# PEER on one Trainium2 core: one instruction for both one-hot matrices, one for both weighted parts, and u summed in PSUM

## The chip, the cores and the metric

The kernel runs on one core of a Trainium2 chip. The metric is the device time of one execution in microseconds (us). Before the change the median of three runs is 2842.26 us (2841.84 to 2842.48).

## The reference, cut to what matters

Two transformer blocks follow each other; the second one ends each of its two layers with PEER, a mixture of 16384 one-row experts. The change lies there.

```python
def peer(h, w_q, sub_keys, u_tab, v_tab):
    xt = h.reshape(-1, PEER_TOKENS, D)
    def chunk_fn(xc):
        T = xc.shape[0]
        q = (xc @ w_q).reshape(T, PEER_HEADS, 2, PEER_QDIM // 2)
        s = jnp.einsum('thcd,hcnd->thcn', q, sub_keys, preferred_element_type=f32)
        sv, si = lax.top_k(s, PEER_TOPK)
        comb = (sv[:, :, 0, :, None] + sv[:, :, 1, None, :]).reshape(T, PEER_HEADS, PEER_TOPK * PEER_TOPK)
        cv, ci = lax.top_k(comb, PEER_TOPK)
        i1 = jnp.take_along_axis(si[:, :, 0], ci // PEER_TOPK, axis=-1)
        i2 = jnp.take_along_axis(si[:, :, 1], ci % PEER_TOPK, axis=-1)
        eidx = i1 * PEER_NKEYS + i2
        w = jax.nn.softmax(cv, axis=-1)
        u = u_tab[eidx]
        a = jax.nn.gelu(jnp.einsum('td,thkd->thk', xc, u, preferred_element_type=f32)) * w
        return jnp.einsum('thk,thkd->td', a.astype(v_tab.dtype), v_tab[eidx])
    return lax.map(chunk_fn, xt).reshape(B, S, D)
```

There are 256 tokens, a model width of 1024, 8 heads, 128 keys for each half and 16 picks a head.

## The kernel before, in words

Weights are streamed. `Stream` loads granules of 128 x 1024 fp32 numbers (512 KB, four raw buffers) over SP's queue. For each granule ACT rounds to fp32r (`wh`, L279), and DVE subtracts to get the rest (`wl`, L284); four such pairs are held, so both run up to three granules ahead of PE. Every product is made of three: wh with the high part of x, wh with the low part, wl with the high part. `Stream.block` hands PE a block and, at the first block of a granule, calls `tick` (one step of each background generator in `bg`), then `ahead` (conversions that are due), then `run_posts` (what was put off to the next granule). That order is the order in DVE's, ACT's and PE's queues; nothing else schedules.

PEER gathers no expert. It computes gelu(u x) for all 16384 experts, in 128 chunks of 128 experts, multiplies by a dense weight W that is zero where an expert was not picked, and multiplies by v, in 128 chunks. Each chunk of u or v is one granule. One layer runs in these stretches (in brackets their begin in layer 0, in us):

- queries and scores, and then `route` as a background generator: top 16 of 128, top 16 of the sums, indices, softmax. Its end writes the tables `i1T`, `i2T`, `wT`, each number twice side by side, tokens along the free axis.
- u chunks 0 to 63 into `G0` (991.6), with `route` still in the background.
- u chunks 64 to 97 into `G1` (1185.2), with `w_gen(0)` in the background.
- v group "a", 30 chunks of `G0` (1308.0).
- u chunks 98 to 127 into `G0` (1391.7), no generator beside them.
- v group "b", 34 chunks (1474.9), with `w_gen(1)` in the background.
- v groups "c" and "d", 64 chunks (1598.0).

`u_chunks` multiplies a chunk by all 256 tokens: for each of 8 blocks a matmul of wh with the high and low parts side by side (512 columns, L1670) and one of wl with the high part (256 columns, L1671). The low sums stand in the other half of the PSUM bank. ACT copies them to `G` (L1675), DVE adds the high half (L1678), and after every second chunk ACT makes the gelu in place (L1681). The two PSUM banks of `pu` (and two of `px` in the first stretch) hold one chunk each and come free with the add.

`w_gen(part, ...)` makes W for 64 of the 128 values of the second key, eight tokens to a tick, 32 ticks and one to end. A tick's `product` (16 small matmuls, L1709) multiplies the one-hot matrix `A` of the first key by the weighted one-hot matrix `B` of the second, in two fp16 parts; `scale` (L1716) multiplies the result of the tick before into `G`; `build` makes E and A by comparing a row of numbers with the tables (L1697, L1698), then the two parts of B (L1701).

`v_chunks` splits two columns of G into a high and a low part (L552 on ACT, L553 `gl` on DVE) and runs 12 matmuls of 512 columns a chunk (L1765). The constant EARLY (34) says how many u chunks run before group "a" and how many v chunks group "b" has.

`lin_t` (L433 to L435) multiplies other layers' weights in three matmuls of 256 columns, wh and wl each under a load of its own; its moving operand in the first MLP is the same tile `x` that u uses.

Of the kernel before, what the change touches and what calls it, by code (L numbers as in the profile page):

```python
# [34 lines left out]
EARLY = 34  # L35
# [293 lines left out]
class TileSum:  # L329
# [35 lines left out]
class Kern:  # L365
# [867 lines left out]
    def ret(self):  # L1233
# [3 lines left out]
        with tc.tile_pool(name="ret", bufs=1, reuse_waits="tile") as mp:  # L1237
            tab = mp.tile([P, 2048], F32, name="tab")
# [221 lines left out]
    def peer(self, layer):  # L1460
# [26 lines left out]
        sv, si = [], []
        for b in range(2):
            t = tp.tile([P, 16, TOPK], F32, name=f"sv{b}")
            sv.append(t)  # L1490
            t = tp.tile([P, 16, TOPK], U32, name=f"si{b}")
            si.append(t)
# [40 lines left out]
        def tile2(shape, dt, name):  # L1533
            r = []
            for b in range(2):
                t = tp.tile(shape, dt, name=f"{name}{b}", bufs=1)
                r.append(t)
            return r

        def route():  # L1540
# [15 lines left out]
            comb = tile2([P, 8, 112], F32, "comb")  # L1556
            sif = tile2([P, 16, TOPK], F16, "sif")
            cv = tile2([P, 8, TOPK], F32, "cv")
            ci = tile2([P, 8, TOPK], U32, "ci")
# [650 lines left out]
```

## Time and profile before

| | before |
|---|---|
| median of 3 runs | 2842.26 us |
| the profiled execution | 2838.77 us |
| its span, first to last instruction | 2837.1 us |
| PE busy | 2729.0 us, 96% |
| PE weight loads busy | 2369.2 us, 84% |
| DVE busy | 2236.7 us, 79% |
| ACT busy | 1485.1 us, 52% |
| POOL busy | 271.4 us, 10% |
| chain that ended last | PE 59%, DVE 33%, issue 5%, ACT 2% |

The profile is one execution. A matmul's duration in it reaches from its start to its modelled end; matmuls overlap, so what one costs is the distance from its start to the next start. On DVE too the next instruction can start a little before the end shown for the one before it. PE's busy share says little for the same reason; the granted clock is at its full level, 2.4 GHz, in all the stretches named above.

### The profile page before, as it was taken

The page shows a single profiled execution, that of the slowest core. Times are in us where ns is not written, and L with a number is a line of the kernel's source. Part 1 is how long each engine was busy: PE and PEld are TensorE (multiplying, and loading weights), DVE is VectorE, ACT ScalarE, POOL GpSimd, SP SyncE. Part 2 cuts the span into 40 slices and gives each one's busy share as a digit, 9 for nine tenths or more (in the row PEclk, how much of TensorE's full clock was granted, in tenths as well). Part 3 has the DMA queues.
Part 4 walks back from the last instruction along what each step waited for, and adds up shares of the span by engine and source line. Part 5 has one row for each costly group of instructions (what it writes and reads, how often), then busy time and mean ns, then how long its engine had stood idle before and what let it go on. Part 6 is the DMA issues. An engine that isn't in the chain of part 4 may idle for free.

```text
span 2837.1 us, 46836 instructions
## 1 busy us (share of the span) xinstructions
PE 2729.0 (96%) x17758; PEld 2369.2 (84%) x17758; DVE 2236.7 (79%) x4398; ACT 1485.1 (52%) x2411; POOL 271.4 (10%) x262
## 2 busy tenths in 40 slices
PE   8999999999999999999999999899999999999998
PEld 7889899898999878888887788778878888877786
DVE  7868977788768899797569755887999895579655
ACT  6557545674545554644553444665546544543444
POOL 2010013000202303000000000212203000000001
PEclk9999999999999999999999999999999999999999
DMA  5648976588554455545554555423455546544663
GB/s 197 223 151 301 320 275 233 183 311 303 188 164 155 138 168 172 185 142 179 188 176 142 178 187 191 131 91 110 132 169 183 168 147 193 186 157 142 192 187 110
DMA packets 143406, 521.04 MB, mean 184 GB/s; under 512 B 15919, under 2 KB 17229, under 8 KB 142669
## 3 DMA queue, kind: packets, MB, share of 16 engines
q1 hardware_dynamic: 142893, 515.96, 55.0%
q8 instruction: 139, 2.28, 0.3%
q10 hardware_dynamic: 288, 2.10, 0.2%
q14 instruction: 86, 0.70, 0.1%
HBM read 516.95 MB, written 1.05 MB: 183 GB/s over the span
## 4 chain that ended last, share of the span: by engine, by line
PE 59%; DVE 33%; issue 5%; ACT 2%; POOL 0%; DMA 0%; SPq 0%; DVEq 0%; ACTq 0%; POOLq 0%
PE vo L1765 18%; DVE wl L284 12%; PE u L1670 6%; PE lin L434 5%; PE lin L433 5%; PE lin L435 5%; PE lin L497 4%; DVE B L1701 3%; PE u L1671 3%; DVE G L1716 3%; PE lin L498 2%; DVE G L1678 2%; DVE E L1697 1%; PE lin L537 1%; PE lin L536 1%
## 5 line engine op out<-in xcount | busy, mean ns | idle before, releaser
L284 DVE TENSOR_TENSOR wl<-raw,wh 128x1024 fp32r<-128x1024 f32 x861 | 1083.8, 1262 | 312.4 <-ACT wh L279 311.8
L279 ACT ACTIVATE wh<-raw 128x1024 fp32r<-128x1024 f32 x861 | 909.9, 1058 | 567.6 <-PE vo L1765 403.4
L1670 PE MATMUL u<-x,wh 128*128 128x512 f32 x2048 | 729.6, 399 | 7.4 <-DVE rawb L1406 0.2
L1671 PE MATMUL u<-x,wl 128*128 128x256 f32 x2048 | 577.0, 282 | 15.0 <-DVE wl L284 13.4
L1670 PEld LDWEIGHTS u<-x,wh 128*128 128x128 f32 x2048 | 384.2, 188 | 101.3 <-DVE G L1678 14.7
L1671 PEld LDWEIGHTS u<-x,wl 128*128 128x128 f32 x2048 | 386.2, 189 | 27.4 <-DVE wl L284 27.2
L1765 PE MATMUL vo<-wh,gl 128*128 128x512 f32 x1008 | 319.3, 398 | 3.8
L1765 PE MATMUL vo<-wh,gh 128*128 128x512 f32 x1008 | 321.2, 400 | 0.0
L1765 PE MATMUL vo<-wl,gh 128*128 128x512 f32 x1008 | 316.0, 394 | 0.0
L433 PE MATMUL lin<-x,wh 128*128 128x256 f32 x920 | 271.0, 295 | 1.9 <-ACT x L555 1.5
L434 PE MATMUL lin<-x,wh 128*128 128x256 f32 x920 | 261.7, 284 | 1.0 <-DVE x L556 0.9
L435 PE MATMUL lin<-x,wl 128*128 128x256 f32 x920 | 260.9, 284 | 0.0
L1765 PEld LDWEIGHTS vo<-wh,gl 128*128 128x128 f32 x1008 | 187.5, 188 | 58.6 <-DVE gl L553 16.9
L1765 PEld LDWEIGHTS vo<-wl,gh 128*128 128x128 f32 x1008 | 189.8, 188 | 44.2
L1765 PEld LDWEIGHTS vo<-wh,gh 128*128 128x128 f32 x1008 | 184.9, 189 | 38.7
L1681 ACT ACTIVATE G<-G 128x512 f32<-128x512 f32 x128 | 80.6, 630 | 229.9 <-DVE G L1678 229.9
L433 PEld LDWEIGHTS lin<-x,wh 128*128 128x128 f32 x920 | 177.4, 193 | 4.0 <-ACT x L555 1.9
L434 PEld LDWEIGHTS lin<-x,wh 128*128 128x128 f32 x920 | 177.4, 193 | 3.1 <-DVE x L556 1.8
L348 POOL TENSOR_TENSOR acc<-sq 128x256 f32<-128x256 f32 x17 | 15.4, 907 | 1690.4 <-ACT sq L337 1690.4
L435 PEld LDWEIGHTS lin<-x,wl 128*128 128x128 f32 x920 | 177.1, 193 | 0.0
L497 PE MATMUL lin<-y,wh 128*128 128x512 f32 x496 | 174.2, 393 | 0.0
L1675 ACT COPY G<-u 128x256 f32<-128x256 f32 x256 | 93.5, 365 | 147.8 <-PE u L1671 147.8
(550 smaller groups left out, 4823.0 us busy)
## 6 DMA issues: line engine op xcount, KB each, us to landing
raw<-in_peer_u SPq DMA_DIRECT2D x256, 512.0 KB, 3.5
raw<-in_peer_v SPq DMA_DIRECT2D x256, 512.0 KB, 3.6
adaw<-in_ada SPq DMA_DIRECT2D x112, 512.0 KB, 6.1
raw<-in_mlp_in SPq DMA_DIRECT2D x64, 512.0 KB, 4.6
raw<-in_mlp_out SPq DMA_DIRECT2D x64, 512.0 KB, 5.4
raw<-in_peer_q SPq DMA_DIRECT2D x32, 512.0 KB, 3.5
raw<-in_sb_qk SPq DMA_DIRECT2D x16, 512.0 KB, 3.7
raw<-in_ret_g SPq DMA_DIRECT2D x16, 512.0 KB, 3.5
```

The costliest lines, as they stand in the source:

```text
L279: k.nc.scalar.activation(h, raw, AF.Copy)
L284: k.nc.vector.tensor_tensor(l, raw, h.bitcast(F32), op=ALU.subtract)
L433: mm(ps, wh, xh, start=start, stop=False)
L434: mm(ps, wh, xl, start=False, stop=False)
L435: mm(ps, wl, xh, start=False, stop=stop)
L497: mm(ps, wh, hl[:, i], start=i == 0, stop=False, **kw)
L1670: mm(p, wh, hx[:, i], start=i == 0, stop=False, skip_group_check=True)
L1671: mm(p[:, 0, :], wl, hh[:, i, :], start=False, stop=i == KT - 1, skip_group_check=True)
L1675: nc.scalar.copy(g, p[:, 1, :])
L1701: nc.vector.tensor_tensor(B[:, j], E, row(wT[:, j, ts, :], PART), op=ALU.mult)
L1716: nc.vector.scalar_tensor_tensor(g, pc[:, c0:c0 + m, :], 1.0 / W_SCALE, g, op0=ALU.mult, op1=ALU.mult)
L1765: mm(vo[2 * b + e], x[:, j, t], w[:, e * 512:(e + 1) * 512], start=fst and m == 0, stop=bool(lst) and m == 2)
```

## The change

- In `u_chunks` the matmul of 512 columns becomes two of 256 with the same weights, and all three add up in the same 256 columns. A PSUM bank now holds two chunks. The copy and the add are gone; the gelu reads PSUM and writes `G`.
- In `w_gen` one comparison makes A and E, as 192 columns for each token: the numbers 0 to 127 and the 64 of the part, against a table `iT` with the first index twice and the second once. One product makes both parts of B, and one `scale` covers all 64 rows also for part 1.
- `G` is one tile of 100 rows; G1 is its first 36, G0 the other 64. EARLY is 36. The routing's tables lie in G1's rows until u is written there.
- The buffers of the running sums (`sq`, `acc`) move to a pool `sums`, which each stage sets.

```diff
-EARLY = 34
+EARLY = 36
...
-        self.iota2 = cp.tile([P, P // 2, 2], F16, name="iota2")
-        nc.vector.tensor_copy(self.iota2.rearrange("p a b -> p (a b)"), self.c("iota"))
+        self.iota3 = cp.tile([P, 2, 3 * PART], F16, name="iota3")
+        for part in range(2):
+            nc.vector.tensor_copy(self.iota3[:, part, :P], self.c("iota"))
+            nc.vector.tensor_copy(self.iota3[:, part, P:], self.c("iota")[:, part * PART:(part + 1) * PART])
...
-        G0 = gp.tile([P, PART, S], F32, name="G0")
+        G = gp.tile([P, EARLY + PART, S], F32, name="G")
+        G0, G1 = G[:, EARLY:, :], G[:, :EARLY, :]
         rt = es.enter_context(tc.tile_pool(name="route", bufs=1, reuse_waits="tile"))
 
-        i1T = rt.tile([P, S, 2], F16, name="i1T")
-        i2T = rt.tile([P, S, 2], F16, name="i2T")
-        wT = rt.tile([P, 2, S, 2], F16, name="wT")
+        iT = rt.tile([P, S, 3, 2], F16, name="iT")
+        wT = rt.tile([P, S, 2, 2], F16, name="wT")
...
+        flat, room = G1.rearrange("p c s -> p (c s)"), [0]
+
+        def table(shape, dt):
+
+            n = math.prod(shape[1:])
+            words = n // 2 if dt == F16 else n
+            t = flat[:, room[0]:room[0] + words]
+            room[0] += words
+            if dt != F32:
+                t = t.bitcast(dt)
+            if len(shape) == 2:
+                return t
+            d = " ".join("abc"[:len(shape) - 1])
+            return t.rearrange(f"p ({d}) -> p {d}", **dict(zip("abc", shape[1:])))
+
+        sv = [table([P, 16, TOPK], F32) for b in range(2)]
...
-                nc.scalar.copy(i1T[:, cols, :], twice(t[:, 0:P]))
-                nc.scalar.copy(i2T[:, cols, :], twice(t[:, P:2 * P]))
-                ws = tp.tile([P, P], F32, name="af0", bufs=1)
+                for i, x in enumerate((t[:, 0:P], t[:, 0:P], t[:, P:2 * P])):
+                    nc.scalar.copy(iT[:, cols, i, :], twice(x))
+                ws = f[b]
                 nc.scalar.activation(ws, t[:, 2 * P:3 * P], AF.Copy, scale=W_SCALE)
-                nc.scalar.copy(wT[:, 0, cols, :], twice(ws))
-                nc.vector.tensor_tensor(wT[:, 1, cols, :], twice(ws), wT[:, 0, cols, :], op=ALU.subtract)
+                nc.scalar.copy(wT[:, cols, 0, :], twice(ws))
+                nc.vector.tensor_tensor(wT[:, cols, 1, :], twice(ws), wT[:, cols, 0, :], op=ALU.subtract)
...
+            kw = dict(skip_group_check=True)
             for c in range(c0, c1):
-                p = pools[c % len(pools)].tile([P, 2, S], F32, name="u")
-                g = dst[:, c - c0, :]
+                if c % 2 == 0:
+                    p = pools[c // 2 % len(pools)].tile([P, 2, S], F32, name="u")
+                o = p[:, c % 2, :]
                 for i in range(KT):
                     wh, wl = self.ws.block(f"peer_u{layer}", P)
-                    mm(p, wh, hx[:, i], start=i == 0, stop=False, skip_group_check=True)
-                    mm(p[:, 0, :], wl, hh[:, i, :], start=False, stop=i == KT - 1, skip_group_check=True)
+                    mm(o, wh, hh[:, i, :], start=i == 0 and c % 2 == 0, stop=False, **kw)
+                    mm(o, wh, hl[:, i, :], start=False, stop=False, **kw)
+                    mm(o, wl, hh[:, i, :], start=False, stop=i == KT - 1, **kw)
                 for f in self.due():
                     f()
                 assert c != 40 or route_at[0] >= 32
-                nc.scalar.copy(g, p[:, 1, :])
-
-                def add(c=c, g=g, p=p):
-                    nc.vector.tensor_tensor(g, p[:, 0, :], g, op=ALU.add)
-                    if c % 2:
-                        g2 = dst[:, c - c0 - 1:c - c0 + 1, :]
-                        nc.scalar.activation(g2, g2, AF.Gelu_apprx_tanh)
-                self.post(add)
-            self.run_posts()
-
-        def w_gen(part, segs, then):
+                if c % 2:
+                    nc.scalar.activation(dst[:, c - c0 - 1:c - c0 + 1, :], p, AF.Gelu_apprx_tanh)
+
+        def w_gen(part, G, then):
 
             TB = 8
             n = S // TB
 
             def build(i):
                 ts = slice(i * TB, (i + 1) * TB)
-                A = ab.tile([P, TB, P // 2, 2], F16, name="A", bufs=2)
-                E = ab.tile([P, TB, PART // 2, 2], F16, name="E", bufs=1)
-                row = lambda x, m: x.unsqueeze(2).to_broadcast([P, TB, m // 2, 2])
-                num = lambda c0, m: self.iota2[:, c0 // 2:(c0 + m) // 2, :].unsqueeze(1).to_broadcast([P, TB, m // 2, 2])
-                nc.vector.tensor_tensor(E, num(part * PART, PART), row(i2T[:, ts, :], PART), op=ALU.is_equal)
-                nc.vector.tensor_tensor(A, num(0, P), row(i1T[:, ts, :], P), op=ALU.is_equal)
-                B = ab.tile([P, 2, TB, PART // 2, 2], F16, name="B", bufs=2)
-                for j in range(2):
-                    nc.vector.tensor_tensor(B[:, j], E, row(wT[:, j, ts, :], PART), op=ALU.mult)
-                live[i] = A.rearrange("p t a b -> p t (a b)"), B.rearrange("p j t a b -> p j t (a b)")
+                A = hp.tile([P, TB, 3 * PART], F16, name="A", bufs=2)
+                shape = [P, TB, 3, PART // 2, 2]
+                split = lambda x, r: x.rearrange("p t (r a b) -> p t r a b", r=r, b=2)
+                nums = self.iota3[:, part, :].rearrange("p (r a b) -> p r a b", r=3, b=2).unsqueeze(1).to_broadcast(shape)
+                nc.vector.tensor_tensor(split(A, 3), nums, iT[:, ts].unsqueeze(3).to_broadcast(shape), op=ALU.is_equal)
+                B = hp.tile([P, TB, 2 * PART], F16, name="B", bufs=2)
+                shape = [P, TB, 2, PART // 2, 2]
+                E = A[:, :, P:].rearrange("p t (a b) -> p t a b", b=2).unsqueeze(2).to_broadcast(shape)
+                nc.vector.tensor_tensor(split(B, 2), E, wT[:, ts].unsqueeze(3).to_broadcast(shape), op=ALU.mult)
+                live[i] = A, B.rearrange("p t (j c) -> p t j c", j=2)
 
             def product(i):
                 A, B = live.pop(i)
                 pt = pw.tile([P, TB, PART], F32, name="w")
                 for t in range(TB):
                     for j in range(2):
-                        mm(pt[:, t, :], A[:, t, :], B[:, j, t, :], start=j == 0, stop=j == 1)
+                        mm(pt[:, t, :], A[:, t, :P], B[:, t, j, :], start=j == 0, stop=j == 1)
                 live[i] = pt
 
             def scale(i):
                 pc = live.pop(i).rearrange("p t c -> p c t")
-                for (G, m, c0) in segs:
-                    g = G[:, 0:m, i * TB:(i + 1) * TB]
-                    nc.vector.scalar_tensor_tensor(g, pc[:, c0:c0 + m, :], 1.0 / W_SCALE, g, op0=ALU.mult, op1=ALU.mult)
+                g = G[:, :, i * TB:(i + 1) * TB]
+                nc.vector.scalar_tensor_tensor(g, pc, 1.0 / W_SCALE, g, op0=ALU.mult, op1=ALU.mult)
 
...
-        self.bg.append(w_gen(0, [(G0, PART, 0)], lambda: prep("a", G0)))
+        self.bg.append(w_gen(0, G0, lambda: prep("a", G0)))
         u_chunks(PART, PART + EARLY, G1, (pu,))
         assert not self.bg
         v_chunks("a", G0, LATE, nxt=("b", late), first=True)
         u_chunks(PART + EARLY, 2 * PART, G0, (pu,))
-        self.bg.append(w_gen(1, [(G1, EARLY, 0), (G0, LATE, EARLY)], lambda: prep("c", G1)))
+        self.bg.append(w_gen(1, G[:, :PART, :], lambda: prep("c", G1)))
         v_chunks("b", late, EARLY)
         assert not self.bg
+        hot.close()
+        self.sums = es.enter_context(tc.tile_pool(name="sums", bufs=1, reuse_waits="tile"))
```

Two places show the new order. On DVE, in the stretch of u chunks 64 and on with W part 0: `wl` is the streamed granule's rest, G is u's result (the row with u) or is scaled by W (the row with w), E, A and B are the one-hot matrices, iT, i1T, i2T and wT the tables. The number behind `waits` only names an engine's counter.

```order
L1716 SCALAR_TENSOR_TENSOR G_10625<-w,G_10625 128x64x8 [waits PE_49]
L1697 TENSOR_TENSOR E<-iota_1190,i2T 128x512 [waits DVE_49]
L1698 TENSOR_TENSOR A<-iota_1190,i1T 128x1024
L1701 TENSOR_TENSOR B<-E,wT 128x512 [waits DVE_49]
L1701 TENSOR_TENSOR B<-E,wT 128x512
L284 TENSOR_TENSOR wl<-raw,wh 128x1024 [waits DMAHW2_49,Activation_49]
L1678 TENSOR_TENSOR G_13341<-u,G_13341 128x256 [waits Activation_49]
```

That is a tick before; the same stretch of DVE's queue in the changed kernel, one tick and the wl on either side of it:

```order
L284 TENSOR_TENSOR wl<-raw,wh 128x1024 [waits DMAHW1_49,Activation_49]
L1723 SCALAR_TENSOR_TENSOR G<-w,G 128x64x8 [waits PE_49]
L1705 TENSOR_TENSOR A<-iota_1193,iT 128x1536
L1709 TENSOR_TENSOR B<-A,wT 128x1024 [waits DVE_49]
L284 TENSOR_TENSOR wl<-raw,wh 128x1024 [waits DMAHW2_49,Activation_49]
```

The add that waited for ACT is gone from DVE, and B stands right behind the instruction on which it waits, where A stood between E and B.

On PE, at the same place, the end of a tick's 16 products (rows with w) and the first block of the next u chunk:

```order
L1709 MATMUL w<-B,A 128x64
L1670 MATMUL u<-x,wh 128x512 [waits DVE_49]
L1671 MATMUL u<-x,wl 128x256
L1670 MATMUL u<-x,wh 128x512
L1671 MATMUL u<-x,wl 128x256
```

The same rows of PE's queue in the changed kernel, two blocks behind a product:

```order
L1717 MATMUL w<-B,A 128x64
L1684 MATMUL u<-x,wh 128x256 [waits Activation_49]
L1685 MATMUL u<-x,wh 128x256
L1686 MATMUL u<-x,wl 128x256
L1684 MATMUL u<-x,wh 128x256
L1685 MATMUL u<-x,wh 128x256
```

Before, the first matmul of each chunk waits for DVE's add; now the first of every second chunk waits for ACT's gelu, and a block is three matmuls.

## Rows read from the trace of the kernel before

**Rows 1.** Busy time by stretch: PE, PEld, DVE, ACT, POOL (count), clock, DMA share, GB/s

```profile
1185.20:1308.00 122.80, 119.20 (x1059) 99.60 (x1057) 121.19 (x229) 54.77 (x86) 0.00 (x0) 1.00 0.44 143
1474.90:1598.00 123.10, 119.89 (x922) 89.44 (x921) 122.53 (x245) 47.06 (x54) 0.00 (x0) 1.00 0.43 140
```

**Rows 2.** Busy time by stretch, the matmuls of L1670 alone (8 to a chunk)

```profile
991.60:1039.90 48.30, 39.86 (x112) 1.00 0.46 151
1039.90:1185.20 145.30, 141.30 (x401) 1.00 0.58 189
1391.70:1474.90 83.20, 83.20 (x240) 1.00 0.58 190
2431.40:2516.20 84.80, 84.77 (x240) 1.00 0.57 186
```

**Rows 3.** Timeline of DVE, one W tick: start us, us, what

```profile
1239.77 0.67 DVE L1716 SCALAR_TENSOR_TENSOR G<-w,G 128x512 f32<-128x512 f32 x1
1240.37 0.41 DVE L1697 TENSOR_TENSOR E<-iota,i2T 128x512 f16<-128x512 f16 x1
1240.70 0.68 DVE L1698 TENSOR_TENSOR A<-iota,i1T 128x1024 f16<-128x1024 f16 x1
1241.30 0.74 DVE L1701 TENSOR_TENSOR B<-E,wT 128x512 f16<-128x512 f16 x2
1241.97 1.21 DVE L284 TENSOR_TENSOR wl<-raw,wh 128x1024 fp32r<-128x1024 f32 x1
1243.11 0.41 DVE L1678 TENSOR_TENSOR G<-u,G 128x256 f32<-128x256 f32 x1
1243.44 0.67 DVE L1716 SCALAR_TENSOR_TENSOR G<-w,G 128x512 f32<-128x512 f32 x1
```

**Rows 4.** Costliest groups, 1185.2 to 1308.0: busy, mean ns | idle before <-releaser

```profile
L1670 PEld LDWEIGHTS u<-x,wh 128*128 128x128 f32 x272 | 51.0, 187 | 18.1 <-DVE G L1678 7.3
```

**Rows 5.** Timeline of PE: narrow matmuls on tile x and on tile oh, 24 apart

```profile
114.32 0.28 PE L435 MATMUL lin<-oh,wl 128*128 128x256 f32 x1
...
117.04 0.28 PE L435 MATMUL lin<-oh,wl 128*128 128x256 f32 x1
...
560.00 0.28 PE L434 MATMUL lin<-x,wh 128*128 128x256 f32 x1
...
562.88 0.28 PE L434 MATMUL lin<-x,wh 128*128 128x256 f32 x1
```

**Rows 6.** Timeline of PE: the first products of W part 0 and u behind them

```profile
1188.08 0.64 PE L1709 MATMUL w<-B,A 128*128 128x64 f16 x16
1188.56 0.47 PE L1670 MATMUL u<-x,wh 128*128 128x512 f32 x1
...
1188.98 0.40 PE L1670 MATMUL u<-x,wh 128*128 128x512 f32 x1
```

**Rows 7.** Timeline of DVE in the routing: L1589 waits for L1588, wl does not

```profile
1082.35 0.29 DVE L1588 SCALAR_TENSOR_TENSOR af<-af,af 128x128 f32<-128x128 f32 x1
1082.68 0.23 DVE L1589 CAST ij<-af 128x128 f16<-128x128 f32 x1
1082.82 1.22 DVE L284 TENSOR_TENSOR wl<-raw,wh 128x1024 fp32r<-128x1024 f32 x1
```

**Rows 8.** Timeline of DVE in v group "b": gl, two scales, E

```profile
1540.61 0.68 DVE L553 TENSOR_TENSOR gl<-G,gh 128x512 fp32r<-128x512 f32 x1
1541.21 0.75 DVE L1716 SCALAR_TENSOR_TENSOR G<-w,G 128x272 f32<-128x272 f32 x2
1541.88 0.41 DVE L1697 TENSOR_TENSOR E<-iota,i2T 128x512 f16<-128x512 f16 x1
```

**Rows 9.** Timeline of DVE in the first u stretch: wl of three granules running

```profile
1000.35 1.22 DVE L284 TENSOR_TENSOR wl<-raw,wh 128x1024 fp32r<-128x1024 f32 x1
...
1003.53 1.21 DVE L284 TENSOR_TENSOR wl<-raw,wh 128x1024 fp32r<-128x1024 f32 x1
...
1007.33 1.21 DVE L284 TENSOR_TENSOR wl<-raw,wh 128x1024 fp32r<-128x1024 f32 x1
```

More of the change, by code (lines that the diff above doesn't have):

```diff
@@ L335, in square @@
     def square(self, i, src):
-        sq = self.k.act.tile([P, S], F32, name="sq", bufs=SQ_BUFS)
+        sq = self.k.sums.tile([P, S], F32, name="sq", bufs=SQ_BUFS)
         self.k.nc.scalar.activation(sq, src, AF.Square)
@@ L346, in add @@
             if i == 1:
-                self.acc = k.act.tile([P, S], F32, name="acc", bufs=2)
+                self.acc = k.sums.tile([P, S], F32, name="acc", bufs=2)
             self.eng.tensor_tensor(self.acc, prev, x, op=ALU.add)
@@ L1481, in peer @@
         px = tk.enter_context(tc.tile_pool(name="px", bufs=2, space=PSUM, reuse_waits="tile"))
-        R = tp.tile([P, KT, 2, WIDE], F32R, name="raw")
         ab = self.lnab[layer * 48 + 32, layer * 48 + 24]
-        self.raw_begin(R, ab)
         keys = G0[:, 56:64, :].rearrange("p c (j k) -> p (c j) k", k=NK)
         nc.scalar.dma_start(keys, self.a[f"peer_k{layer}"])
[L1487 to L1492, printed above, removed]
+        flat, room = G1.rearrange("p c s -> p (c s)"), [0]
[11 more added lines that the diff above has]
+        sv = [table([P, 16, TOPK], F32) for b in range(2)]
+        si = [table([P, 16, TOPK], U32) for b in range(2)]
+        R = tp.tile([P, KT, 2, WIDE], F32R, name="raw")
+        self.raw_begin(R, ab)
         work, route_at = [], [0]
@@ L1531, in evac_q, with tile2 @@
             self.later(score, 2)
[L1533 to L1538, printed above, removed]
+        def tile2(shape, dt):
+            return [table(shape, dt) for b in range(2)]
         def route():
@@ L1555, in route @@
                 yield
[L1556 to L1559, printed above, removed]
+            comb = tile2([P, 8, 112], F32)
+            sif = tile2([P, 16, TOPK], F16)
+            cv = tile2([P, 8, TOPK], F32)
+            ci = tile2([P, 8, TOPK], U32)
             for b in range(2):
@@ L1574, in route @@
             for j in range(2):
-                ix.append(tile2([P, P], F32, f"ix{j}"))
+                ix.append(tile2([P, P], F32))
             ij = []
+            u = table([P, 8, TOPK], U32)
+            f = tile2([P, P], F32)
             for b in range(2):
-                t = tp.tile([P, 2, P], F16, name=f"ij{b}", bufs=1)
+                t = table([P, 2, P], F16)
                 ij.append(t)
-                u = tp.tile([P, 8, TOPK], U32, name="ai", bufs=1)
-                f = [tp.tile([P, P], F32, name=f"af{i}", bufs=1) for i in range(2)]
                 cb = ci[b].rearrange("p h k -> p (h k)")
@@ L1594, in route @@
                 nc.vector.tensor_tensor(t[:, 1, :], f[0], f[1], op=ALU.subtract)
-            oh = tile2([P, 8, TOPK, TOPK], F16, "oh")
-            it = tp.tile([P, TOPK, TOPK], F16, name="iota16", bufs=1)
+            oh = tile2([P, 8, TOPK, TOPK], F16)
+            it = table([P, TOPK, TOPK], F16)
             nc.vector.tensor_copy(it, iota[:, :TOPK].unsqueeze(2).to_broadcast([P, TOPK, TOPK]))
@@ L1733, in peer @@
         ab = es.enter_context(tc.tile_pool(name="ab", bufs=1, reuse_waits="tile"))
-        G1 = ab.tile([P, EARLY, S], F32, name="G1")
+        hot = ExitStack()
+        hp = hot.enter_context(tc.tile_pool(name="hot", bufs=1, reuse_waits="tile"))
         pv = es.enter_context(tc.tile_pool(name="pv", bufs=1, space=PSUM, reuse_waits="tile"))
@@ L1833, in nsa @@
         with ExitStack() as es:
-            mp = es.enter_context(tc.tile_pool(name="nsa", bufs=1, reuse_waits="tile"))
+            mp = self.sums = es.enter_context(tc.tile_pool(name="nsa", bufs=1, reuse_waits="tile"))
             kh = mp.tile([P, KT, S], F32R, name="kh")
@@ L2133, in body @@
         k.ps_es = k.open_ps()
+        sums = ExitStack()
+        k.sums = sums.enter_context(tc.tile_pool(name="sums", bufs=1))
         b1 = ExitStack()
```

7 lines of the change are left out of this document (5 added, 2 removed).

## The prediction, made before the changed kernel had run

> **What bounds the kernel now.** I read the page first: PE is busy 96% of the span, DVE 79%, ACT 52%, and the chain that ended last is 59% PE and 33% DVE. The next view is the busy time by stretch, cut at the stage borders of layer 0's PEER (layer 1's stretches differ by 0.4 us or less, save one that is named). In the stretch of u chunks 64 to 97, where W part 0 is built, 122.8 us pass for 34 chunks and DVE is busy for 121.19 of them. In v group "b", where W part 1 is built, DVE is busy 122.53 of 123.10 us [rows 1]. Both are held by DVE. Where nothing is built beside u, PE sets the pace: 240 wide matmuls are 30 chunks of 8, so a chunk takes 83.2/30 = 2.77 us in layer 0 and 84.8/30 = 2.83 us in layer 1. The first stretch is mixed: its first 14 chunks (112 wide matmuls) take 48.3 us, 3.45 us each, the other 50 take 145.3 us, 2.91 each [rows 2].
>
> The timeline of DVE inside the W stretch gives what each instruction costs from its start to the next start: scale 0.60, E 0.33, A 0.60, the two B together 0.67, wl 1.14, G add 0.33, then the next scale [rows 3]. That is 3.67 us a tick, without a gap. PE's own tick is shorter: 16 products take 0.48 us, and the first u pair behind them 0.42 us where the others take 0.35 [rows 6], so a build costs PE 0.55 us, and 2.8 + 0.55 = 3.35. PE makes up the difference by waiting, 18.1 us in the stretch before the loads of u's weights, and most of what the trace can name of it is on the G add [rows 4], which frees the PSUM bank.
>
> **The change part by part.**
>
> *Three narrow matmuls for two.* A u block was 512 + 256 columns under two weight loads and becomes three times 256 under three loads: 8 more matmuls and 8 more loads a chunk, 2048 in all. The same form, on the same tile x, runs in the first MLP: 24 of them from 560.00 to 562.88 us, 2.88 us [rows 5]. The nearest other row, on tile oh, needs 114.32 to 117.04, 2.72 us [rows 5]. I take 2.88, since operand and form are the same; 2.72 is the bound below, and 2.95 (about as far above 2.88 as 2.88 lies above the mean of 2.77 and 2.83) the one above, an estimate. PE gets slower here by 0.05 to 0.11 us a chunk.
>
> *The G add and the copy go.* 256 adds leave DVE, 0.33 us each, and 256 copies leave ACT, which is not near a bound. The gelu now reads PSUM and frees the bank; there are two banks of two chunks each, so PE has one pair (5.8 us) before it needs the bank back. I cost that at nothing: gelu has 5.8 us for an instruction that takes 0.6 us. If ACT held it back longer, PE would show a wait on gelu at the first matmul of every other chunk.
>
> *E joins A, two B become one.* A step from 512 to 1024 elements costs 0.60 - 0.33 = 0.27 us [rows 3], so A with 1536 elements costs 0.87 and B with 1024 costs 0.60. But A stood between E and B, and now B follows the instruction that it waits for. A dependent instruction starts 0.03 us behind the end of the one before it (1082.35 + 0.29 to 1082.68), an independent one 0.08 us ahead of it (1240.37 + 0.41 to 1240.70), so the wait costs 0.11 us [rows 3, 7]. A and B cost 0.87 + 0.11 + 0.60 = 1.58 us, against 0.33 + 0.60 + 0.67 = 1.60: the merging by itself gives nothing. The Trainium skill (VectorE: DVE Perf Modes, section The DRAIN you can't avoid) says otherwise, that a semaphore after every copy "costs nothing extra here"; by it A and B would cost 1.47. The rows here show the 0.11, so I keep it.
>
> *G as one tile.* In group "b" one scale replaces two, which cost 0.67 from the first to E [rows 8], by one of 0.60. The tables keep their shapes, so the routing's operations cost what they did. On ACT, the load of the keys gets a wait on PE in front of the first instruction of the new stage; PE's last matmuls of the stage before are what that stage's statistics wait for too, so I cost it at nothing (a microsecond for each layer if it were late).
>
> *EARLY 36.* Two chunks move from the last u stretch to the W stretch, two v chunks from "a" to "b", at their own pace. A build needs 33 ticks either way.
>
> **The sum, for one layer.**
> - *First u stretch.* Its first 14 chunks alternate between 3.18 and 3.80 us (single and double top-16 work), as DVE's wl instructions do [rows 9]. Without the add they would take 2.85 and 3.47; PE's 2.88 lifts the first. A pair goes from 6.98 to 6.35, seven pairs give -4.4. The other 50 chunks take 145.3 and have a floor of 50 x 2.88 = 144.0; I give 1 us for stalls that stay: 0.
> - *W stretch.* DVE's tick becomes 1.14 + 0.60 + 1.58 = 3.32. PE's is 2.88 + 0.55 = 3.43, and PE becomes the bound. 32 ticks with products and 4 chunks without give 32 x 3.43 + 4 x 2.88 = 121.3, where 34 chunks took 122.8 and the two that are new here took 5.6 elsewhere: -7.1.
> - *Last u stretch*, 28 chunks of 2.88: +3.1 in layer 0, +1.4 in layer 1.
> - *Group "b"*: DVE's tick was 1.14 + 0.30 (half a gl) + 0.67 + 1.60 = 3.71 and becomes 1.14 + 0.30 + 0.60 + 1.58 = 3.62, still above PE: 32 x 0.09 = -2.9.
>
> Two layers: 2 x (-4.4 - 7.1 - 2.9) + 4.5 = -24.3 us. The profiled execution took 2838.8 us (span 2837.1 and 1.7 around it) and would take 2814.5; it lies 3.5 us under the median of the runs, so the forecast is 2842.3 - 24.3 = **2818 us**. With the pace at 2.95 about 228 PE-bound chunks cost 16 us more: 2834.
>
> **The rivals.**
> - *The wait moves.* In the W stretch the add was only the last of several waits, and B, the scale's PSUM bank or wl take its place at 3.67 us. For it: DVE had no gap, so its queue is long. Against: the queue loses 0.35 us and needs only 3.32. The W stretch would take 32 x 3.67 + 4 x 2.88 = 129.0 instead of 121.3, 15.4 us for both layers: 2833.
> - *The merged instructions lose their pace.* A and B read patterns of more levels and might go one element at a time, as the 4-byte wl does: 1.14 us for 1024 against 0.33 for 256 (the add) is 0.54 us for 512 more [rows 3]. A would cost 1.68 + 0.11, B 1.14. The W tick is then 4.67 and the one of "b" 4.97: 32 x 4.67 + 4 x 2.88 = 161.0, 39.7 us over the forecast, and 32 x (4.97 - 3.62) = 43.2, for each layer. That gives 2818 + 166 = 2984. It makes the kernel slower from where A and B cost 0.25 us more than 1.58 (0.14 x 32 in W, where PE hides 0.11, and 0.25 x 32 in "b" are 12.5 us, a layer's gain). Against: flattened, table and output have the pairs of neighbours that they had.
> - *Narrow matmuls at a slower pace yet.* Over 228 chunks the gain is gone at 2.88 + 24.3/228 = 2.99 us. The rows on x speak against it.
> - *The wait between A and B is free.* Then only "b" gains, as W is PE's: 0.11 x 32 x 2 = 7 us, 2811. The rows on dependent pairs speak against it [rows 7]. The Trainium skill's section named above speaks for it.
> - *Narrow matmuls at 2.72*, as on oh. Then the first stretch gains 4.7 + 7, W is DVE's (32 x 3.32 + 4 x 2.72 = 117.1, -11.3), the last stretch gains 2.2, "b" 2.9: 28 for each layer, 2786.
>
> **How the numbers follow.** Chances: the forecast (2806 to 2830) 0.62; the wait moves 0.14; the free wait 0.08; 2.72 us 0.06; a pace near or over 2.99, 0.06; merged instructions at half pace 0.04. The range of 2803 to 2837 holds the forecast, the moved wait, the free wait and a pace of 2.95, and leaves out the outer cases. A measurement of this kernel can tell about 0.2%, 5.7 us, from no change. Under 2836.6 lie the first four cases and some of the fifth, less those moved waits that cost more than reckoned: 0.85 faster. Between 2836.6 and 2848: 0.08. Above: 0.07, half pace and a pace over 3.0.
>
> **What would show it.** In the profile after: u's matmuls at 0.12 us from start to start and 2.88 us a chunk in the last u stretch; a W tick of 3.43 us with gaps on DVE and none on PE; A at some 0.95 us and B 0.03 us behind its end; "b" with DVE full at 3.62 us a tick; the first 14 chunks in 44 us. A W tick of 3.67, or a B of over 1 us, or a last u stretch of other than 80.6 us for 28 chunks would prove the step wrong that gave it.

## The result, and the profile after

The changed kernel takes 2811.12 us, the median of four runs (2809.20 to 2814.26); the kernel before, beside it, takes 2842.37 (2841.84 to 2843.88). The ratio is 0.989, with a 95% interval of 0.9873 to 0.9907: 31 us, or 1.1%, less. The forecast was 2818 with a range of 2803 to 2837. The profiled execution took 2810.98 us, 27.8 less than the one before; the rest of the 31 is that the profiled execution of before lay 3.5 us under its own median, while the one of the changed kernel lay at it.

The first and fourth part of the page of the changed kernel (busy time, share of the span, instructions; then the chain of work that ended last):

```profile
PE 2725.7 (97%) x19806; PEld 2481.0 (88%) x19806; DVE 2139.1 (76%) x3825; ACT 1415.7 (50%) x2159; POOL 269.4 (10%) x262
...
PE 77%; DVE 17%; issue 3%; ACT 2%; POOL 0%; DMA 0%; SPq 0%; ACTq 0%; DVEq 0%; POOLq 0%
```

PE's share of the chain went from 59% to 77%, DVE's from 33% to 17%. Where that happened stands in the view by stretch (PE, PEld, DVE, ACT, POOL busy, clock, DMA share, GB/s), the W stretch and group "b" of layer 0, which answer to [rows 1]:

```profile
1181.07:1302.24 121.17, 121.17 (x1378) 119.79 (x1377) 112.24 (x131) 47.43 (x55) 0.00 (x0) 1.00 0.51 157
1460.96:1583.84 122.88, 121.85 (x946) 92.69 (x945) 119.57 (x148) 49.20 (x56) 0.00 (x0) 1.00 0.48 151
```

In the W stretch PE is now busy for all of the 121.17 us, and DVE for 112.24 where it had been full. The stretch holds 36 chunks now, where it held 34 in 122.80. In "b", too, 36 chunks take 122.88, where 34 took 123.10; DVE is still busy for 119.57 of them.

The u matmuls by stretch (the first matmul of each block, 8 to a chunk: PE, PEld busy, clock, DMA share, GB/s) answer to [rows 2]; first 14 chunks, the next 50, the last u stretch of layer 0:

```profile
991.10:1036.40 45.30, 31.90 (x112) 21.53 (x113) 1.00 0.52 162
1036.40:1181.07 144.67, 113.28 (x401) 76.82 (x401) 1.00 0.60 190
1380.33:1460.96 80.63, 63.39 (x224) 42.81 (x223) 1.00 0.58 183
```

28 chunks in 80.63 us are 2.88 each. The timeline of PE shows the pace directly (start us, us, what): from a matmul to the 24th after it, in the last u stretch, 2.88 us, as [rows 5] had it on x; and a tick's products in the W stretch, 0.48 us, with 0.43 us for the first block of u behind them (three matmuls; the other blocks take 0.36), which answers to [rows 6]:

```profile
1183.95 0.64 PE L1717 MATMUL w<-B,A 128*128 128x64 f16 x16
1184.43 0.36 PE L1684 MATMUL u<-x,wh 128*128 128x256 f32 x1
...
1184.86 0.28 PE L1684 MATMUL u<-x,wh 128*128 128x256 f32 x1
...
1396.88 0.28 PE L1684 MATMUL u<-x,wh 128*128 128x256 f32 x1
...
1399.76 0.28 PE L1684 MATMUL u<-x,wh 128*128 128x256 f32 x1
```

One W tick of DVE, which answers to [rows 3] and [rows 7]:

```profile
1239.45 0.69 DVE L1723 SCALAR_TENSOR_TENSOR G<-w,G 128x512 f32<-128x512 f32 x1
1240.06 0.95 DVE L1705 TENSOR_TENSOR A<-iota,iT 128x1536 f16<-128x1536 f16 x1
1241.05 0.69 DVE L1709 TENSOR_TENSOR B<-A,wT 128x1024 f16<-128x1024 f16 x1
1241.65 1.22 DVE L284 TENSOR_TENSOR wl<-raw,wh 128x1024 fp32r<-128x1024 f32 x1
1242.88 0.69 DVE L1723 SCALAR_TENSOR_TENSOR G<-w,G 128x512 f32<-128x512 f32 x1
```

The tick is 1242.88 - 1239.45 = 3.43 us. A and B need 0.99 + 0.60 = 1.59. B starts at 1241.05, A ends at 1240.06 + 0.95 = 1241.01: B waits for A's end. The wl needs 1.14, so 0.1 us of the 1.23 before the next scale is a gap: DVE waits for PE now (a tick's products end at 1242.20 + 0.64 = 1242.84, and the scale starts at 1242.88). PE in turn waits for nothing at the weights of u, where it had lost 18.1 us [rows 4] (the costliest groups in the W stretch: busy, mean ns, idle before):

```profile
L1684 PEld LDWEIGHTS u<-x,wh 128*128 128x128 f32 x288 | 55.0, 191 | 0.0
```

Two ticks of DVE in group "b", late in it, answer to [rows 8]:

```profile
1547.66 0.68 DVE L1723 SCALAR_TENSOR_TENSOR G<-w,G 128x512 f32<-128x512 f32 x1
1548.26 0.95 DVE L1705 TENSOR_TENSOR A<-iota,iT 128x1536 f16<-128x1536 f16 x1
1549.24 0.69 DVE L1709 TENSOR_TENSOR B<-A,wT 128x1024 f16<-128x1024 f16 x1
1549.85 1.22 DVE L284 TENSOR_TENSOR wl<-raw,wh 128x1024 fp32r<-128x1024 f32 x1
1550.99 0.68 DVE L553 TENSOR_TENSOR gl<-G,gh 128x512 fp32r<-128x512 f32 x1
1551.59 0.69 DVE L1723 SCALAR_TENSOR_TENSOR G<-w,G 128x512 f32<-128x512 f32 x1
...
1554.92 0.68 DVE L1723 SCALAR_TENSOR_TENSOR G<-w,G 128x512 f32<-128x512 f32 x1
```

They take 1554.92 - 1547.66 = 7.26 us, 3.63 each, without a gap: DVE-bound, as forecast (3.62). But the stretch as a whole is not. The products' starts on PE, the first, the 16th, and the last of the 32 ticks:

```profile
1463.74 0.64 PE L1717 MATMUL w<-B,A 128*128 128x64 f16 x16
...
1514.04 0.64 PE L1717 MATMUL w<-B,A 128*128 128x64 f16 x16
...
1571.78 0.64 PE L1717 MATMUL w<-B,A 128*128 128x64 f16 x16
```

The first 15 ticks take 50.30 us, 3.35 each, which is PE's own pace; the other 16 take 57.74, 3.61 each on average (they alternate between some 3.35 and 3.9). In the kernel before only the first three ticks ran at PE's pace:

```profile
1477.65 0.64 PE L1709 MATMUL w<-B,A 128*128 128x64 f16 x16
...
1487.72 0.64 PE L1709 MATMUL w<-B,A 128*128 128x64 f16 x16
1491.42 0.74 PE L1709 MATMUL w<-B,A 128*128 128x64 f16 x11
```

They took 10.07 us, 3.36 each, and the fourth 3.70. That is what the forecast had missed, and the timeline of DVE at the start of "b" suggests why. Before (PE's first matmul of "b" is at 1474.87):

```profile
1475.47 0.42 DVE L1678 TENSOR_TENSOR G<-u,G 128x256 f32<-128x256 f32 x1 [2.35 <-ACT G L1675]
1475.81 0.41 DVE L1697 TENSOR_TENSOR E<-iota,i2T 128x512 f16<-128x512 f16 x1
```

And the changed kernel (PE's first matmul of "b" is at 1460.96):

```profile
1458.12 0.95 DVE L1705 TENSOR_TENSOR A<-iota,iT 128x1536 f16<-128x1536 f16 x1
```

Before, the last add of u waited 2.35 us in DVE's queue for ACT's copy, and the first build began 0.9 us after PE had entered "b". Without adds it begins 2.8 us ahead of PE: 3.8 us earlier.

### The profile page after: what moved, and what is told of

Its sections match the earlier page's. It is cut to its first block, busy times and chain, and to the rows that moved or that the text cites. A ratio compares the mean times of both kernels' runs of the same rounds, so it can differ in the third digit from the quotient of the medians.

```text
span 2809.3 us, 50000 instructions
## 1 busy us (share of the span) xinstructions
PE 2725.7 (97%) x19806; PEld 2481.0 (88%) x19806; DVE 2139.1 (76%) x3825; ACT 1415.7 (50%) x2159; POOL 269.4 (10%) x262
## 4 chain that ended last, share of the span: by engine, by line
PE 77%; DVE 17%; issue 3%; ACT 2%; POOL 0%; DMA 0%; SPq 0%; ACTq 0%; DVEq 0%; POOLq 0%
PE vo L1773 20%; PE u L1684 8%; PE u L1686 8%; PE u L1685 8%; DVE wl L284 6%; PE lin L434 5%; PE lin L433 5%; PE lin L435 5%; PE lin L497 4%; PE lin L498 2%; DVE A L1705 1%; PE w L1717 1%; PE lin L537 1%; PE lin L536 1%; PE lin L538 1%
## 5 line engine op out<-in xcount | busy, mean ns | idle before, releaser
L1684 PE MATMUL u<-x,wh 128*128 128x256 f32 x2048 | 585.0, 286 | 0.2 <-DVE rawb L1409 0.2
L1685 PE MATMUL u<-x,wh 128*128 128x256 f32 x2048 | 579.0, 283 | 0.0
L1686 PEld LDWEIGHTS u<-x,wl 128*128 128x128 f32 x2048 | 392.3, 192 | 7.3 <-DVE wl L284 7.3
L1684 PEld LDWEIGHTS u<-x,wh 128*128 128x128 f32 x2048 | 392.5, 192 | 0.4 <-issue 0.3
L1685 PEld LDWEIGHTS u<-x,wh 128*128 128x128 f32 x2048 | 392.5, 192 | 0.1
L1691 ACT ACTIVATE G<-u 128x512 f32<-128x512 f32 x128 | 76.6, 599 | 247.7 <-PE u L1686 247.4
```

What stands on the lines that cost most here:

```text
L1684: mm(o, wh, hh[:, i, :], start=i == 0 and c % 2 == 0, stop=False, **kw)
L1685: mm(o, wh, hl[:, i, :], start=False, stop=False, **kw)
L1686: mm(o, wl, hh[:, i, :], start=False, stop=i == KT - 1, **kw)
L1691: nc.scalar.activation(dst[:, c - c0 - 1:c - c0 + 1, :], p, AF.Gelu_apprx_tanh)
```

## The experiments

The theory after this: the u part of the change carries the gain; merging A and E, and B, is worth next to nothing; in "b" the gain is larger than forecast since DVE starts 3.8 us earlier and PE runs at its own pace until that lead (how far DVE is ahead of what PE needs from it) is used up. The rival for "b": the ticks themselves, or the two chunks that EARLY 36 adds, are cheaper than reckoned.

**u wide again.** The u part of the change is undone, all else stays.

```diff
-                    mm(o, wh, hh[:, i, :], start=i == 0 and c % 2 == 0, stop=False, **kw)
-                    mm(o, wh, hl[:, i, :], start=False, stop=False, **kw)
-                    mm(o, wl, hh[:, i, :], start=False, stop=i == KT - 1, **kw)
+                    mm(p, wh, hx[:, i], start=i == 0, stop=False, skip_group_check=True)
+                    mm(p[:, 0, :], wl, hh[:, i, :], start=False, stop=i == KT - 1, skip_group_check=True)
...
+                nc.scalar.copy(g, p[:, 1, :])
...
+                    nc.vector.tensor_tensor(g, p[:, 0, :], g, op=ALU.add)
```

> The changed kernel with u as before (512 + 256 columns, copy on ACT, add on DVE); the merged A and B, the one G and EARLY 36 stay. Theory (the u part carries the gain; group b's extra gain is DVE's early start, which the adds take away again): first u stretch 193.5 us, W stretch 32 x 3.65 + 4 x 2.8 = 128, last u stretch 77.6 and 79.2, group b 125.8; for both layers +22 us over the changed kernel, 2833. Rival (the merged instructions made group b faster than reckoned): group b stays at 122.9, 2827.

2833.3 us (2831.69 to 2835.08; ratio to before 0.9971, 0.9959 to 0.9983). The W stretch and group "b" of layer 0:

```profile
1185.03:1313.05 128.02, 125.16 (x1090) 104.52 (x1089) 122.79 (x169) 57.99 (x91) 0.00 (x0) 1.00 0.46 147
...
1469.12:1595.44 126.32, 124.59 (x947) 92.27 (x945) 122.58 (x152) 49.50 (x57) 0.00 (x0) 1.00 0.46 146
```

128.02 and 126.32: the W stretch loses 6.9 us, "b" 3.4. As the theory had it: with the adds back, "b" loses its extra gain, though A, B and the scale are the merged ones. What it still gains on before (8 us by the medians, 5 by the profiled executions) is for the most part the one scale for two in "b", 2.4 us a layer (36 chunks of before would have taken 123.10 + 2 x 2.79 = 128.7), and a wide u pace of 2.77 us in layer 1, where it had been 2.83.

**A, E and B apart again.** u stays narrow; E, A and two B are four instructions with their old tables.

```diff
-                nc.vector.tensor_tensor(split(A, 3), nums, iT[:, ts].unsqueeze(3).to_broadcast(shape), op=ALU.is_equal)
...
-                nc.vector.tensor_tensor(split(B, 2), E, wT[:, ts].unsqueeze(3).to_broadcast(shape), op=ALU.mult)
...
+                nc.vector.tensor_tensor(E, num(part * PART, PART), row(i2T[:, ts, :], PART), op=ALU.is_equal)
+                nc.vector.tensor_tensor(A, num(0, P), row(i1T[:, ts, :], P), op=ALU.is_equal)
...
+                for j in range(2):
+                    nc.vector.tensor_tensor(B[:, j], E, row(wT[:, j, ts, :], PART), op=ALU.mult)
```

> The changed kernel with E, A and two B as four instructions and their old tables; u stays narrow and summed in PSUM. Theory (merging is worth nothing by itself): A and what belongs to it cost 1.60 us for 1.58, the W stretch stays PE-bound at 121.2, group b 122.9 to 123.6; 2811 to 2813. Rival (the merged instructions carry the gain that group b showed beyond the forecast): group b 125.8, 2817.

2812.45 us (2812.08 to 2813.89; ratio 0.9899, 0.9884 to 0.9914). Group "b":

```profile
1459.76:1583.07 123.31, 122.09 (x947) 93.22 (x945) 121.05 (x210) 49.19 (x56) 0.00 (x0) 1.00 0.47 151
```

0.4 us a layer in "b", and 121.18 us in the W stretch as with the merged ones: the first half of the change's name moves the time by less than a measurement can tell. It is not what made "b" faster.

**The scale between A and B.** The same instructions in another order.

```diff
                 nc.vector.tensor_tensor(split(A, 3), nums, iT[:, ts].unsqueeze(3).to_broadcast(shape), op=ALU.is_equal)
+                if mid is not None and mid >= 0:
+                    scale(mid)
                 B = hp.tile([P, TB, 2 * PART], F16, name="B", bufs=2)
...
-                if i >= 2:
-                    scale(i - 2)
                 if i < n:
-                    build(i)
+                    build(i, i - 2)
                 else:
+                    scale(n - 2)
                     scale(n - 1)
```

> The changed kernel with the scale of an earlier tick put between A and B, so that B no longer follows the instruction it waits for. Theory (a dependent pair costs 0.11 us more than an independent one): DVE's full tick in group b 3.62 -> 3.51 us, over PE's 3.36 by 0.15 in place of 0.26; less DVE's 3.7 us of lead that is 1.3 us over PE's pace for 0.15 x 33 in place of 4.9, so group b 119.3; the W stretch unchanged; 2804. Rival (the wait between dependent instructions is free): group b 122.9, 2811.

2804.61 us (2804.17 to 2804.94; ratio 0.9869, 0.9854 to 0.9885). DVE late in "b", and the stretch by engine:

```profile
1559.82 0.95 DVE L1705 TENSOR_TENSOR A<-iota,iT 128x1536 f16<-128x1536 f16 x1
1560.68 0.68 DVE L1725 SCALAR_TENSOR_TENSOR G<-w,G 128x512 f32<-128x512 f32 x1
1561.28 0.68 DVE L1711 TENSOR_TENSOR B<-A,wT 128x1024 f16<-128x1024 f16 x1
1561.88 1.21 DVE L284 TENSOR_TENSOR wl<-raw,wh 128x1024 fp32r<-128x1024 f32 x1
...
1566.83 0.95 DVE L1705 TENSOR_TENSOR A<-iota,iT 128x1536 f16<-128x1536 f16 x1
```

```profile
1461.86:1581.10 119.24, 119.24 (x947) 93.16 (x945) 116.95 (x148) 49.19 (x56) 0.00 (x0) 1.00 0.47 156
```

A now costs 0.86 us to the next start, where it cost 0.98 with B behind it; the scale starts 0.09 us before A's end. Two ticks take 1566.83 - 1559.82 = 7.01 us, 3.51 each. "b" falls to 119.24, and 26 ticks run at PE's pace. The wait between dependent instructions has its price, 0.11 to 0.12 us, and where DVE sets the pace it is worth 3.6 us a layer. The W stretch, where PE sets it, stayed at 121.2. This also says why merging alone gave next to nothing: the two larger instructions save 0.13 us a tick (0.87 + 0.60 against 1.60) and the wait between them takes 0.11 of it back. With the wait out of the way, "b" is 4.1 us shorter than with the four instructions (119.24 against 123.31), and those had no such wait: A stood between E and B.

**DVE held at the start of "b".** One copy of one column, no other work.

```diff
         u_chunks(PART + EARLY, 2 * PART, G0, (pu,))
+        held = ab.tile([P, 1], F32, name="held")
+        nc.vector.tensor_copy(held, G0[:, PART - EARLY - 1, 0:1])
```

> The changed kernel with one tiny copy on DVE between the last u stretch and group b, of one column of the last gelu's result: it adds no work, but DVE can no longer build ahead before the last u chunk is done. Theory (group b's extra gain is that early start): the first A of group b starts after PE's first matmul of it in place of 2.8 us before, the ticks at PE's pace (3.35) fall from 14 to 4, group b 125.8; 2817. Rival (the extra gain lies in the ticks themselves, or in the two chunks that EARLY 36 adds): group b 122.9, 2811.

2818.75 us (2817.57 to 2819.28; ratio 0.992, 0.9906 to 0.9933). DVE at the start of "b", then the stretch:

```profile
1461.57 0.15 DVE L1829 COPY held<-G 128x1 f32<-128x1 f32 x1 [3.59 <-ACT G L1691]
1461.64 0.95 DVE L1705 TENSOR_TENSOR A<-iota,iT 128x1536 f16<-128x1536 f16 x1
```

```profile
1460.74:1587.02 126.28, 124.57 (x947) 92.27 (x946) 122.32 (x152) 49.19 (x56) 0.00 (x0) 1.00 0.45 147
```

The first build starts 0.9 us after PE's entry, as before the change, three ticks run at PE's pace instead of 15, and "b" takes 126.28: 3.4 us a layer for an instruction of 0.15 us. Twelve ticks at some 3.63 instead of 3.35 are the same 3.4 us. This settles where the extra gain of "b" comes from; the instructions of a tick and EARLY were the same here.

**The last u stretch wide.** Only its 28 chunks are as before, with copies and adds (`u_wide` is the `u_chunks` of the kernel before).

```diff
-        u_chunks(PART + EARLY, 2 * PART, G0, (pu,))
+        u_wide(PART + EARLY, 2 * PART, G0, (pu,))
```

> The changed kernel with the 28 chunks of the last u stretch as before (512 + 256 columns, copy and add). Theory (wide is the faster pace for PE, but the last adds hold DVE at the start of group b): last u stretch 77.6 to 79.2 in place of 80.6, group b 126.3 in place of 122.9, so the one takes back the other: +0.4 to +2 us a layer, 2812 to 2815. Rival (the adds hold nothing): group b stays at 122.9 and the kernel gains the pace, 2805 to 2808.

2812.74 us (2810.48 to 2814.72; ratio 0.9905, 0.9889 to 0.9922). The last u stretch and "b" of layer 0:

```profile
1380.21:1457.86 77.65, 77.65 (x449) 68.52 (x448) 44.55 (x54) 43.80 (x68) 0.00 (x0) 1.00 0.63 190
1457.86:1584.21 126.35, 124.60 (x946) 92.29 (x945) 122.62 (x152) 49.49 (x57) 0.00 (x0) 1.00 0.46 146
```

Three us gained in one stretch, 3.5 lost in the next. The changed kernel once more, on the same chip:

> The changed kernel once more, beside the others on the same chip: every theory has it at 2811, group b 122.9 and the last u stretch 80.6.

2812.04 us (2810.97 to 2813.25), with 80.6 and 122.9 in the two stretches: no difference between the two kernels that can be measured.

**The last u stretch wide but for its end.** With the scale between A and B; the last four chunks are narrow.

```diff
-        u_chunks(PART + EARLY, 2 * PART, G0, (pu,))
+        u_wide(PART + EARLY, 2 * PART - 4, G0, (pu,))
+        u_chunks(2 * PART - 4, 2 * PART, G0[:, LATE - 4:, :], (pu,))
```

> The scale between A and B, and the last u stretch wide as before for 24 of its 28 chunks, the last four narrow, so that no add stands at DVE when group b begins. Theory: 24 x 0.05 to 0.11 us less in the last u stretch, 78.0 to 79.4, group b 119.2 as with the scale between alone: 2799 to 2802. Rival (the adds take the lead all the same): group b 122 or more, 2804 to 2807.

2799.25 us (2797.91 to 2801.39; ratio 0.9854, 0.9837 to 0.987). The same two stretches:

```profile
1382.74:1460.81 78.07, 78.07 (x481) 70.25 (x480) 45.91 (x55) 43.05 (x65) 0.00 (x0) 1.00 0.64 189
1460.81:1580.07 119.26, 119.26 (x947) 93.16 (x945) 116.95 (x148) 49.19 (x56) 0.00 (x0) 1.00 0.48 156
```

78.07 and 119.26: both gains hold. This kernel is 13 us below the changed kernel on the same chip, and 5 us below the one with the scale between A and B alone, which ran on another chip.

**Building ahead.** If the lead of DVE is worth time, more of it should be worth more. Three kernels tried it, all with E, A and B apart (their tables are smaller, so three buffers for A and B fit) and EARLY 34. In the first, group "b" builds one tick further ahead, in front of the scale, and its generator begins beside the last two u chunks:

```diff
+            if part:
+                build(0)
+                yield
             for i in range(n + 1):
                 if i >= 1:
                     product(i - 1)
-                if i >= 2:
-                    scale(i - 2)
-                if i < n:
-                    build(i)
+                if part:
+                    if i + 1 < n:
+                        build(i + 1)
+                    if i >= 2:
+                        scale(i - 2)
...
-        u_chunks(PART + EARLY, 2 * PART, G0, (pu,))
+        u_chunks(PART + EARLY, 2 * PART - 2, G0, (pu,))
         self.bg.append(w_gen(1, G[:, :PART, :], lambda: prep("c", G1)))
+        u_chunks(2 * PART - 2, 2 * PART, G0[:, LATE - 2:, :], (pu,))
```

> The changed kernel with E, A and two B as four instructions (their tables are smaller), EARLY 34 and three buffers for A and B; in group b DVE builds one tick further ahead, the first build lies beside the last u chunks. Theory (group b gains as much as DVE is ahead of PE at its start): one tick more of lead, 3.4 us, is used up at 0.27 us a tick; with EARLY 34 group b has 34 chunks, 33 x 3.36 + 2.8 = 113.7 and what is over PE's pace 33 x 0.27 less 7.1 us of lead, 1.8: 115.5; the last u stretch has 30 chunks, 86.4, group a 83.7, the W stretch 115.5 for 34 chunks; 2806. Rival (the lead is limited by something else, the PSUM banks of the products or wh on ACT, so building ahead moves nothing): group b 119.3 for 34 chunks, 2812.

2812.13 us (2809.71 to 2813.84; ratio 0.9903, 0.9886 to 0.9919): nothing gained. "b" took 116.9 us, not 115.5. The edit also moved the first products from the second chunk of "b" to the first, 2.8 us earlier in PE's queue. DVE's first build began 8.6 us before the first product, where it was 5.6 with four instructions and no building ahead, so a lead was left; it bought no more ticks at PE's pace (14, where four instructions without it had 15). The second kernel puts the products back:

```diff
             if part:
+                yield
                 build(0)
                 yield
-            for i in range(n + 1):
+                build(1)
+                yield
+            for i in range(1 if part else 0, n + 1):
```

> As the kernel that builds ahead, but the first products of group b stand at its second chunk again (there they had moved to its first, which took back 2.8 us of the lead that the early build gave): one build of 1.60 us lies beside the last u chunk, nothing else moves. Theory (what counts is how much of DVE's queue is done when PE needs the next thing from it): group b with 34 chunks takes 117.7 us without the early build (122.9 less two chunks of 2.79, and 0.4 for the four instructions) and 116.1 with it; the whole kernel 2809. Rival (PSUM's two banks or gl hold PE whatever is built early): 116.9 or more, 2811 or more.

2811.23 us (2808.96 to 2813.17; ratio 0.9896, 0.988 to 0.9913), "b" at 117.3 and not 116.1: the theory missed again. Last u stretch and "b" together take 203.7 us in both kernels, so where the first products stood made no difference. What PE's weight loads waited for in "b" (busy, mean ns, idle before and its releasers):

```profile
L1786 PEld LDWEIGHTS vo<-wh,gl 128*128 128x128 f32 x136 | 25.0, 188 | 9.2 <-DVE gl L553 3.9
L1716 PEld LDWEIGHTS <-A 128*128 128x128 f16 x512 | 16.7, 98 | 10.7 <-DVE G L1722 7.2 <-issue 2.5 <-DVE wl L284 0.6
```

The products wait for the scale, which frees their PSUM bank and now stands behind a build. The third kernel has the scale first:

```diff
-                    if i + 1 < n:
-                        build(i + 1)
                     if i >= 2:
                         scale(i - 2)
+                    if i + 1 < n:
+                        build(i + 1)
```

> As the kernel before it (one build ahead, products where they were), but DVE makes the scale first and the build for two ticks later behind it. In the kernel before, PE waited at the products for the scale, which stood behind a build in the same tick, so the place that the build had left was taken by the scale. Theory (PE waits for the last instruction of DVE's tick that it needs; with the build two ticks ahead that is now the scale at its head, 1.60 us earlier in the queue): six more ticks at PE's 3.35, group b 115.7 for 34 chunks, 2808. Rival (gl, which neither order moves, holds PE by itself): group b 117.3 as before it, 2811.

2811.74 us (2806.76 to 2812.56; ratio 0.9891, 0.9874 to 0.9907), "b" at 117.1: the rival. The same two rows:

```profile
L1786 PEld LDWEIGHTS vo<-wh,gl 128*128 128x128 f32 x136 | 24.9, 188 | 10.9 <-DVE gl L553 5.6
L1716 PEld LDWEIGHTS <-A 128*128 128x128 f16 x512 | 16.7, 98 | 8.9 <-issue 7.2 <-DVE wl L284 0.6 <-DVE B L1708 0.6
```

Now the products hardly wait for DVE, but PE's wait for gl has grown from 3.9 to 5.6 us, and 15 ticks run at PE's pace, no more than without building ahead. "b" in the second and the third kernel (PE, PEld, DVE, ACT, POOL busy, clock, DMA share, GB/s):

```profile
1468.18:1585.53 117.35, 116.20 (x923) 88.31 (x921) 116.49 (x203) 46.77 (x53) 0.00 (x0) 1.00 0.47 150
1468.54:1585.67 117.13, 115.02 (x923) 88.24 (x921) 116.40 (x203) 46.79 (x53) 0.00 (x0) 1.00 0.47 150
```

DVE is busy for all but 0.9 and 0.7 us, so the 116.1 and 115.7 that were expected lay under what DVE did in the stretch. An early build should have taken 1.60 us of that work out of "b". The yardstick for it, 117.7 us for 34 chunks without an early build, was only reckoned and not run; against it 0.4 to 0.6 us are left. A possible reason, argued from the order of DVE's queue and not shown: a build that is done early also stands ahead of every gl, so DVE starts one build sooner and has one build more to do before the first gl. Whether gl posted two chunks ahead would lift the limit was not tried.

## Why the prediction was right, and where it was off

For each layer, stretch by stretch, the two chunks moved by EARLY counted at their own pace (layer 0 / layer 1 where they differ; measured from the starts of the chunks' first matmuls in both traces):

| term | forecast, us | measured, us |
|---|---|---|
| first u stretch | -4.4 | -3.7 / -3.5 |
| W stretch | -7.1 | -7.1 / -7.3 |
| last u stretch | +3.1 / +1.4 | +3.0 / +1.5 |
| group "b" | -2.9 | -5.8 / -5.9 |
| both layers | -24.3 | -28.9, from unrounded times |

Outside PEER the profiled execution is 1.0 us longer; the time from the last matmul of the v groups of layer 0 to the first u matmul of layer 1 differs by that much from trace to trace (262.5 us in the changed kernel, 260.8 in the one with the last u stretch wide, whose code there is the same), so it is not put down to the change.

Of the 7 us between 2818 and 2811, 4.6 lie in the stretches of the table: "b" gained 5.9 us more than forecast in the two layers and the first u stretch 1.6 less, so two errors in part cancelled. Some 3.5 are that the profiled execution of before lay under its median, and the 1.0 goes the other way.

- *The narrow pace.* Right: 2.88 us a chunk on x, to the digit, wherever PE runs free. Neither the 2.72 of the other row nor 2.95 came up. The price, 3.0 us in the last u stretch of layer 0, was paid as forecast.
- *The W stretch.* Right: PE is the bound, a tick takes 3.43 us, DVE has the gaps, and the wait on the add went without another in its place. The rival that the wait moves is out.
- *A and B.* Right: 1.59 us for a forecast of 1.58, B 0.03 us behind A's end. The merged instructions keep their pace (the rival at half pace is out), and apart they take the kernel to 2812.45.
- *The first u stretch.* The three wl that answer to [rows 9]:

```profile
999.88 1.22 DVE L284 TENSOR_TENSOR wl<-raw,wh 128x1024 fp32r<-128x1024 f32 x1
...
1002.74 1.21 DVE L284 TENSOR_TENSOR wl<-raw,wh 128x1024 fp32r<-128x1024 f32 x1
...
1006.19 1.22 DVE L284 TENSOR_TENSOR wl<-raw,wh 128x1024 fp32r<-128x1024 f32 x1
```

  Steps of 2.86 and 3.45 us, for a forecast of 2.85 and 3.47 on DVE. But the first 14 chunks took 45.3 us, not 44: the gain of 0.63 to 0.7 us a pair was counted for seven pairs and came in five. The first four chunks take 3.32, 3.32, 2.96 and 3.19 us, where they took 3.26, 3.23, 2.87 and 3.36: in the trace of before PE waits for no add there, and the narrow pace costs the first three 0.06 to 0.09 us each. The other 50 gave 0.5 us in layer 0 and 0.2 in layer 1, for a forecast of none. One of them, near the 50th, still takes 3.45 us in both layers: six matmuls of the routing (L1646, 1140.11 to 1140.65 in layer 0) stand inside it on PE.
- *Group "b"* is the step that was mis-sized: "DVE's tick was ... 3.71 and becomes ... 3.62, still above PE: 32 x 0.09 = -2.9". It measured -5.8 to -5.9. The tick was right (3.63), and by itself it is worth 2.4 us (126.3 in the held kernel against 128.7). What was left out is the start: with the adds, DVE's queue stood still until u was done; without them DVE enters "b" 3.8 us further ahead of PE, and 15 ticks, not 3, ran at PE's 3.35. The held kernel took exactly this away, 3.4 us a layer. The part on the adds priced what they cost DVE in time and not what waiting in them had kept from starting.
- *The number 2811.* The rival of a free wait between A and B gave 2811, and the kernel takes 2811, but that is not how it came about. The Trainium skill (VectorE: DVE Perf Modes, section The DRAIN you can't avoid) says of its own copies, of which it does not tell whether one waits for another, that a semaphore after each costs nothing extra; here a B that waits for A starts 0.03 us after its end, a scale that doesn't 0.09 us before it, and taking the wait away brought 3.6 us a layer in "b". A total that fits a rival is no evidence for it: its own step, B's start, spoke against it.

## What to carry to other kernels

An instruction that waits in an in-order queue can cost more than its own time: ask what stands behind it, and how far ahead of the bound engine that queue could otherwise enter the next stage. Where the ticks of two engines are near each other (here 3.35 and 3.63 us), such a lead sets the pace for many ticks (here 3.8 us more of it gave 12 more ticks at the faster pace), and it is lost again by one tiny dependent instruction at the border. Between two dependent instructions on the bound engine put one that depends on neither; between two on an engine that waits anyway it changed nothing here (the W stretch).

## What the runs showed of the hardware that was not expected

- The same code has two paces, by stretch. In the last u stretch a wide u chunk took 2.77 us in layer 0 and 2.83 in layer 1 before [rows 2], and 2.77 in both layers with only the last u stretch wide (77.65 us for 28 in layer 0, 77.7 in layer 1). Groups "c" and "d" together took 172.7 us in most traces and 173.4 in some. No run here shows what decides it; the narrow u chunks had 2.88 in every trace.
